# Reading a scatter table back on another queue, and loading the last expert pair one step later

## The chip, the cores and the metric

The kernel runs on one core of a Trainium2 chip. A core has a matrix engine (TensorE, PE in the profile, with its weight loads as PEld), VectorE (DVE), ScalarE (ACT), GpSimd (POOL) and SyncE (SP), which run side by side and wait for each other through semaphores. Transfers between the chip's memory (HBM) and the core's own memory are issued from SP, ACT or POOL and carried by 16 DMA engines. The metric is the device time of one execution in microseconds (us). Lower is better.

## The reference, cut to what matters

One decoder layer over 512 tokens of width 1024: two token-mixing groups, an output projection and a layer norm, and then a mixture of experts with a second layer norm. All that the change touches lies in the experts:

```python
def _hier_moe(h, w_group, b_group, w_expert, b_expert, w1_exp, w3_exp, w2_exp):
    # top-1 of 4 groups, then top-2 of the 8 experts inside that group: `gates`
    ...
    for gi in range(N_GROUPS):
        hid = jax.nn.silu(jnp.einsum('nd,edf->nef', tok, w1_exp[gi])) * jnp.einsum('nd,edf->nef', tok, w3_exp[gi])
        out = out + jnp.einsum('nef,efd->nd', hid * gates[:, gi, :, None], w2_exp[gi])
...
    h = _layer_norm(DEEPNORM_ALPHA * h + ffn, ln2_g, ln2_b)
```

There are 32 experts of width 256, in f32. An expert's w1 and w3 are 2 MB together (its "first weights", tile a), its w2 is 1 MB (its "second weights", tile b). All 96 MB are read from HBM once.

## The kernel before, in words

The 32 experts are worked off as 16 pairs, p = 0 to 15. A pair has 128 slots, 64 for each of its experts, that hold the tokens routed to it. For each pair `gather` fetches the slots' rows by an indirect DMA on GpSimd's queue, `rows` turns them with TensorE and scales them (L1019 on VectorE, L1021 on ScalarE), `ups` multiplies them with the first weights, `hidden` makes silu times product times gate (L1225 on ScalarE, L1226 on VectorE), `turn` turns the result (L1231), and `down` multiplies it with the second weights, in two halves.

What comes out of a pair goes back to its tokens in one of two ways. Pairs 0 to 12 go through `second`: the result is scattered by an indirect DMA on GpSimd's queue (L1316) into a table in HBM, ydram, with two rows for a token. Pairs 13 to 15 (from `LATE_` = 13) go through `combine`: TensorE spreads the result over the tokens, and VectorE adds it to them from the banks (L1214). ydram is read back once, by `back` (L1386), in four DMAs of 1 MB into two tiles a, RT[0] to RT[3], and `gained_rows` (L1394) adds its eight blocks, in 16 additions of 128x512, 12 on VectorE and 4 on GpSimd. RT's tiles are those in which the first weights of pair 13 lay, so they come free with `ups(13)`.

The last pair, `last_pair`, first sums the rows of its second weights (`row_sums`, L1450 on VectorE and L1454 on ScalarE); the sums serve the means of the last layer norm, so that the norm can begin before the last product is out.

The weights come on SP's queue, in the order in which the code issues them. First weights have seven tiles, second weights six. `load_a` and `load_b` load one expert's in one DMA; `load_pair` loads the first weights of two experts in eight DMAs of 512 KB, quarter by quarter. `loads_b(p)` loads the second weights of pair p + 3, at the end of `second(p)`, and for p = 12 those of the last pair, in four halves. Before the change the first weights of the last pair, experts 30 and 31, are issued in step p = 12 (L1333), before `second(11)` issues the second weights of experts 28 and 29.

Two further loads are SP's: the second norm's gain and bias (L1327, at p = 13), of which GpSimd scales the gain (L1328).

The instructions of an engine run in the order of the built program, which a scheduler makes from the code and its dependencies; each waits for the semaphores that stand with it. DMAs of SP's and ACT's queues take turns on eight semaphores, DMAHW0 to DMAHW7, and those of GpSimd's queue on eight others, DMASW0 to DMASW7. A DMA that comes to a semaphore waits, on its issuing engine, until the DMA that held it before has landed.

Of the kernel before, what the change touches and what calls it, by code (L numbers as in the profile page):

```python
# [185 lines left out]
def layer(ctx: ExitStack, tc: tile.TileContext, xT, xt, wb, wad, pc, wla, al, gl, cst, cst2, cst3, abias, wout,  # L186
          lnp, lnt, wr, br, wex, out):
    nc = tc.nc
    PE, V, S, P, SP = nc.tensor, nc.vector, nc.scalar, nc.gpsimd, nc.sync
# [6 lines left out]
    ydram = pdr.tile([1024, 1024], F32, name="ydram")  # L196
# [12 lines left out]
    def T(n, *where):  # L209
        return Buf(n, where or (base,))  # L210
# [20 lines left out]
    def tp(o, i):  # L231
        return inorder(PE.transpose(o, i, late("ident")))  # L232
# [629 lines left out]
    LQ = 15  # L862
# [9 lines left out]
    def load_pair(e, n):  # L872

        for j in (e, e + 1):
            wa_[j] = wa_[j - n] if n else area(f"a{SA[j % len(SA)]}").t
        for q in range(0, 4096, 4096 // HV):
            for j in (e, e + 1):
                SP.dma_start(wa_[j][:, q:q + 4096 // HV], wex[j, :, q:q + 4096 // HV])
# [349 lines left out]
    def turn(pt):  # L1228
        for f in range(2):
            tp(pt[:, 128 * f:128 * f + 128], hd.f[:, 128 * f:128 * f + 128])  # L1230
        S.activation(hdT.f, pt[:, 0:256], AF.Copy)  # L1231
# [61 lines left out]
    def experts_first():  # L1293


        for i in range(4):
            if f"g{i}" not in MODE:
                gains1(i, (P, V))
        after(SP.dma_start(rdram, RR.f), g1, "rows first")
        BB[6] = area("b6")  # L1300
        GA.append(T(1024, BB[6]))
        HTs.append(T(1024, BB[6]))
        P.memset(GA[1].f, 0.0)
        gather(2)
        strict[0], last[1] = True, last[0]

        def second(p):
            Y = YY[p % 2]
            for n in range(2):
                py = B[4 + n]  # L1310
                down(p, n, py)
                if n:
                    V.tensor_copy(Y.g[:, 512:1024], py)
                else:
                    S.activation(Y.g[:, 0:512], py, AF.Copy)
            P.indirect_dma_start(out=ydram, out_offset=bass.IndirectOffsetOnAxis(ap=IDY.i[:, p:p + 1], axis=0),  # L1316
                                 in_=Y.g, in_offset=None, bounds_check=1023, oob_is_err=False)
            loads_b(p)

        for p in range(15):  # L1320
            ph = B[0] if p % 2 or p >= LATE_ else B[6]
            ups(p, HTs[p % 2], ph)
            if p == 13:
                L2.append(area(f"a{SA[4]}"))
                G2 = T(2048, L2[0])
                for j in range(2):
                    SP.dma_start(G2.f[:, 1024 * j:1024 * j + 1024], lnp[2 + j:3 + j, :].to_broadcast([128, 1024]))  # L1327
                P.tensor_scalar(G2.f[:, 0:1024], G2.f[:, 0:1024], -12.0 * K_ ** 5, None, op0=OP.mult)  # L1328
                L2.append(G2)
            late_a = []  # L1330
            if p < HP:
                load_pair(2 * p + 7, 7)
            if LQ <= p + 3 < 16:  # L1333
                load_pair(2 * p + 6, 0)
            for e in range(2 * p + 7, min(2 * p + 9, 2 * LQ) if p >= HP else 0):
                if p < 4 or e == 2 * p + 7:
                    load_a(e, SA)
                else:
                    late_a.append(e)
            hidden(p, ph)  # L1340
            if p < LATE_:
                rows(p + 1, dst=HTs[(p + 1) % 2])
                if p + 3 < 16:
                    gather(p + 3)
                if p > 0:
                    second(p - 1)
                turn(B[3])
            else:
                cbs = lambda k: combine(p - 1, CBS[k]) if p > LATE_ else None
                if p == LATE_:  # L1350
                    second(p - 1)
                    combining()
                if p == 14:
                    back()
                cbs(0)
                turn(B[3])
                cbs(1)
                py = bank((4, 5))
                down(p, 0, py)
                parts(0, py)  # L1360
                cbs(2)
                rows(p + 1, (0,), HTs[(p + 1) % 2])
                cbs(3)
                rows(p + 1, (1,), HTs[(p + 1) % 2])
                if p + 3 < 16:
                    gather(p + 3)
                ot(p)
                py = bank((4, 5))
                down(p, 1, py)
                parts(1, py)  # L1370
                loads_b(p)
            for e in late_a:
                load_a(e, SA)
        gained_rows()
        last_pair(SB, None)

    RT = []

    def back():

        for j in range(2):
            t = T(4096, area(f"a{SA[5 + j]}"))
            for q in range(2):
                RT.append(Part(t, 2048 * q, 2048))
        for i in range(4):
            S.dma_start(RT[i].f, ydram.rearrange("(t r) d -> t (r d)", r=2)[128 * i:128 * i + 128, :])  # L1386

    def gained_rows():
        for i in range(4):
# [239 lines left out]
```

## Time and profile before

| what | us |
|---|---|
| median of 3 runs (772.22 to 775.95) | 775.69 |
| the profiled execution, device time | 777.46 |
| its span from first to last instruction | 775.7 |
| PE busy | 669.7 (86%) |
| PEld busy | 422.9 (55%) |
| DVE busy | 429.2 (55%) |
| ACT busy | 250.2 (32%) |
| POOL busy | 191.3 (25%) |

Of the chain of work that ended last, 53% of the span is PE, 22% DMA and 20% DVE. The first 500 us are token mixing and routing; the experts' steps fill the rest up to some 750 us, and the last norm and the stores the end. From 500 us on the DMA engines are busy nearly throughout, at some 420 GB/s, up to a gap near 690 to 700 us; the weights' last bytes land near 732 us. The steps of the expert pairs can be told in the rows by their waits for DMAs of in_wex, the experts' weights. Busy shares over the whole span say little here: what counts is which wait ends last from 690 us on.

### The profile page before, as it was taken

How to read it: one execution, taken by the hardware profiler on the slowest of the kernel's cores; microseconds unless marked ns; L12 is line 12 of the kernel's file. 1: busy time of each engine (PE TensorE's matmuls, PEld its weight loads, DVE VectorE, ACT ScalarE, POOL GpSimd, SP SyncE). 2: the span in 40 equal slices, each digit the busy share in tenths (PEclk: the TensorE clock that was granted, in tenths of full speed). 3: DMA queues.
4: the chain of work that ended last, by engine and by line, in shares of the span. 5: the costliest groups of instructions: out<-in, count | busy, mean ns of one | idle time of the engine just before them, and what ended most of it. 6: DMA issues, size and time to landing. Idle time of an engine off the chain costs nothing.

```text
span 775.7 us, 9701 instructions
## 1 busy us (share of the span) xinstructions
PE 669.7 (86%) x3420; PEld 422.9 (55%) x3420; DVE 429.2 (55%) x1243; ACT 250.2 (32%) x525; POOL 191.3 (25%) x194
## 2 busy tenths in 40 slices
PE   8988988889889899899999996599998897768780
PEld 2766866777778577667767776233332242223240
DVE  4489579869877985663444498622121121105586
ACT  4333224143333436462453432123131131101230
POOL 3133332262253120310310233511121121100332
PEclk9989999989898999999999996699999899889795
DMA  9611000000000112431538446399999999979602
GB/s 326 246 55 55 28 28 28 27 28 28 28 28 19 50 55 82 125 129 38 207 114 330 185 151 270 118 363 423 422 426 423 423 421 428 423 292 381 270 3 112
DMA packets 28484, 147.18 MB, mean 190 GB/s; under 512 B 5113, under 2 KB 5625, under 8 KB 20492
## 3 DMA queue, kind: packets, MB, share of 16 engines
q1 hardware_dynamic: 23676, 134.61, 44.5%
q0 software_dynamic: 4032, 7.42, 2.6%
q10 hardware_dynamic: 720, 4.46, 1.5%
q8 instruction: 29, 0.48, 0.3%
q14 instruction: 27, 0.22, 0.1%
HBM read 138.38 MB, written 15.36 MB: 198 GB/s over the span
## 4 chain that ended last, share of the span: by engine, by line
PE 53%; DMA 22%; DVE 20%; issue 2%; ACT 1%; POOL 1%; ACTq 0%; SPq 0%; DVEq 0%; POOLq 0%
PE bank L229 49%; DMA a<-in_wex 17%; PE bank L232 4%; DVE base L586 2%; DMA a<-ydram 2%; DVE base L587 2%; DVE a L147 1%; DMA b<-in_wex 1%; DVE base L585 1%; DVE b L603 1%; DMA ydram<-x,base 1%; DVE a L460 1%; DMA a<-in_xT 1%; DVE base L242 1%; DVE base L147 1%
## 5 line engine op out<-in xcount | busy, mean ns | idle before, releaser
L229 PE MATMUL bank<-a,b 128*128 128x512 f32 (+2 forms) x1112 | 286.9, 456 | 12.5 <-DMA a<-in_wex 11.8
L229 PEld LDWEIGHTS bank<-a,b 128*128 128x128 f32 (+1 forms) x1112 | 158.3, 175 | 95.2 <-issue 50.2
L229 PE MATMUL bank<-b,base 128*64 128x512 f32 (+1 forms) x412 | 95.1, 501 | 18.7 <-DMA b<-in_wex 15.1
L337 POOL TENSOR_TENSOR b<-b,b 128x1024 fp32r<-128x1024 f32 x22 | 52.4, 2380 | 131.6 <-ACT b L336 131.2
L229 PE MATMUL bank<-a,base 128*64 128x512 f32 (+3 forms) x308 | 75.6, 570 | 3.8 <-DMA a<-in_wex 3.0
L1226 DVE SCALAR_TENSOR_TENSOR base<-bank,base 128x256 f32<-128x256 f32 x16 | 7.7, 484 | 127.1 <-ACT base L1225 127.0
L229 PEld LDWEIGHTS bank<-b,base 128*64 128x64 f32 (+1 forms) x412 | 41.9, 163 | 58.7 <-issue 42.3
L229 PE MATMUL bank<-a 128*128 128x128 f32 (+4 forms) x248 | 55.6, 333 | 5.4 <-DVE base L243 2.6
L229 PEld LDWEIGHTS bank<-a,base 128*64 128x64 f32 (+2 forms) x308 | 25.9, 143 | 46.0 <-issue 35.3
L1225 ACT ACTIVATE base<-bank 128x256 f32<-128x256 f32 x16 | 6.2, 386 | 135.7 <-PE bank L229 135.7
L229 PEld LDWEIGHTS bank<-a 128*128 128x128 f32 (+1 forms) x248 | 36.0, 190 | 18.2 <-issue 5.3
L229 PE MATMUL bank<-a,a 128*128 128x128 f32 (+2 forms) x200 | 42.6, 346 | 1.4 <-DVE base L243 1.1
L232 PEld LDWEIGHTS bank<-base 128*128 128x128 f32 x156 | 18.3, 145 | 34.3 <-issue 17.8
L229 PEld LDWEIGHTS bank<-a,a 128*128 128x128 f32 x200 | 32.2, 213 | 8.7 <-issue 5.1
L232 PE MATMUL bank<-base 128*128 128x128 f32 x156 | 30.3, 294 | 6.4 <-DVE base L689 5.8
L229 PE MATMUL bank<-base 128*128 128x36 f32 (+4 forms) x136 | 28.3, 344 | 8.0 <-DVE base L1062 2.8
L232 PE MATMUL bank<-base,a 128*128 128x128 f32 x168 | 31.6, 289 | 0.0
L229 PE MATMUL bank<-b,a 128*128 128x128 f32 x192 | 30.1, 299 | 1.7 <-DVE a L645 1.1
L336 ACT ACTIVATE b<-b 128x1024 fp32r<-128x1024 f32 x25 | 26.3, 1055 | 13.7 <-PE bank L229 6.7
L229 PEld LDWEIGHTS bank<-b,a 128*128 128x128 f32 x192 | 27.1, 212 | 4.0 <-DVE a L645 1.9
L1316 POOL DMA_INDIRECT ydram<-x,base x13 | 13.1, 1011 | 64.7 <-ACT base L1231 55.6
L520 DVE CUSTOM_DVE_ANT_0 a<-bank,a 128x512 f32<-128x512 f32 (+3 forms) x32 | 15.6, 489 | 21.0 <-PE bank L232 13.7
(310 smaller groups left out, 1006.1 us busy)
## 6 DMA issues: line engine op xcount, KB each, us to landing
a<-in_wex SPq DMA_DIRECT2D x28, 2048.0 KB, 32.1
b<-in_wex SPq DMA_DIRECT2D x30, 1024.0 KB, 23.6
b<-in_wb SPq DMA_DIRECT2D x25, 512.0 KB, 3.3
a<-in_wex SPq DMA_DIRECT2D x16, 512.0 KB, 9.6
ydram<-base SPq DMA_DIRECT2D x1, 4096.0 KB, 15.1
a<-ydram ACTq DMA_DIRECT2D x4, 1024.0 KB, 12.6
x<-in_wout SPq DMA_DIRECT2D x6, 512.0 KB, 4.7
a<-in_xT SPq DMA_DIRECT2D x8, 256.0 KB, 5.6
```

What stands on the lines that cost most here:

```text
L147: ins = f(*args, **kw)
L229: return inorder(PE.matmul(o, l, r, start=start, stop=stop, skip_group_check=True))
L232: return inorder(PE.transpose(o, i, late("ident")))
L242: V.tensor_tensor(t, y, y, op=OP.mult)
L336: S.activation(hi.f, raw.f, AF.Copy)
L337: (V if 0 < k < 4 else P).tensor_tensor(lo.f, raw.f, hi.g, op=OP.subtract)
L460: V.scalar_tensor_tensor(r.f, r.f, pcol(f"rk{hp}"), k2.f, op0=OP.mult, op1=OP.mult)
L520: V.tensor_tensor_reduce(scs[h].f[:, 0:n], ps[:, 0:n], DT.f[:, 512 - n:512], 1.0, -3e38, op0=OP.add, op1=OP.max, accum_out=mx[:, h:h + 1])
L585: V.stream_shuffle(zt3[:, :, s + 1:], tc3[:, :, s + 1:], [16 * (j // 16) + s for j in range(32)])
L586: V.tensor_tensor(zt3[:, :, s + 1:], zt3[:, :, s + 1:], z3[:, :, s:s + 1].to_broadcast([128, 8, 15 - s]), op=OP.mult)
L587: V.tensor_tensor(z3[:, :, s + 1:], z3[:, :, s + 1:], zt3[:, :, s + 1:], op=OP.add)
L1316: P.indirect_dma_start(out=ydram, out_offset=bass.IndirectOffsetOnAxis(ap=IDY.i[:, p:p + 1], axis=0), in_=Y.g, in_offset=None, bounds_chec ...
```

## The change

Three edits. `load_pair` for the last pair moves from ahead of `hidden(12)` to behind `second(11)`, so that experts 28's and 29's second weights stand ahead of it on SP's queue. `back` moves from step 14 to step 13, right behind `second(12)` and `combining`, and its four DMAs are issued on GpSimd's queue, not ScalarE's. And `loads_b(p)` at the end of steps 13 and 14 goes; for those two p it loads nothing.

```diff
@@ experts_first, loop over p
-            if LQ <= p + 3 < 16:
-                load_pair(2 * p + 6, 0)
...
                 if p > 0:
                     second(p - 1)
+                if p == LQ - 3:
+                    load_pair(2 * LQ, 0)
                 turn(B[3])
...
                 if p == LATE_:
                     second(p - 1)
                     combining()
-                if p == 14:
                     back()
...
                 parts(1, py)
-                loads_b(p)
@@ back
-            S.dma_start(RT[i].f, ydram.rearrange("(t r) d -> t (r d)", r=2)[128 * i:128 * i + 128, :])
+            P.dma_start(RT[i].f, ydram.rearrange("(t r) d -> t (r d)", r=2)[128 * i:128 * i + 128, :])
```

What the built programs make of it is seen at three places. On SP's queue, from the second weights of experts 26 and 27 (tiles b_6) on, this stood before (1024 columns are a quarter of an expert's first weights, 2048 an expert's second weights):

```order
L882 DMA b_6_4147<-in_wex 128x2048 [waits DMAHW0_49,PE_49]
L882 DMA b_6_4149<-in_wex 128x2048 [waits DMAHW2_49,PE_49]
L878 DMA a_3_4170<-in_wex 128x1024 [waits DMAHW4_49]
L878 DMA a_5_4171<-in_wex 128x1024 [waits DMAHW5_49,PE_49]
L878 DMA a_3_4170<-in_wex 128x1024 [waits DMAHW7_49]
L878 DMA a_5_4171<-in_wex 128x1024 [waits DMAHW0_49]
L878 DMA a_3_4170<-in_wex 128x1024 [waits DMAHW1_49]
L878 DMA a_5_4171<-in_wex 128x1024 [waits DMAHW2_49]
L878 DMA a_3_4170<-in_wex 128x1024 [waits DMAHW3_49]
L878 DMA a_5_4171<-in_wex 128x1024 [waits DMAHW4_49]
L882 DMA b_6_4214<-in_wex 128x2048 [waits DMAHW5_49,PE_49]
L882 DMA b_6_4216<-in_wex 128x2048 [waits DMAHW6_49,PE_49]
```

and this stands now:

```order
L882 DMA b_6_4147<-in_wex 128x2048 [waits DMAHW7_49,PE_49]
L882 DMA b_6_4149<-in_wex 128x2048 [waits DMAHW0_49,PE_49]
L882 DMA b_6_4204<-in_wex 128x2048 [waits DMAHW1_49,PE_49]
L882 DMA b_6_4206<-in_wex 128x2048 [waits DMAHW2_49,PE_49]
L878 DMA a_3_4208<-in_wex 128x1024 [waits DMAHW3_49]
L878 DMA a_5_4209<-in_wex 128x1024 [waits DMAHW4_49]
L878 DMA a_3_4208<-in_wex 128x1024 [waits DMAHW5_49]
L878 DMA a_5_4209<-in_wex 128x1024 [waits DMAHW6_49]
L878 DMA a_3_4208<-in_wex 128x1024 [waits DMAHW7_49]
L878 DMA a_5_4209<-in_wex 128x1024 [waits DMAHW0_49]
L878 DMA a_3_4208<-in_wex 128x1024 [waits DMAHW1_49]
L878 DMA a_5_4209<-in_wex 128x1024 [waits DMAHW2_49]
```

Before, SP's DMAs skip the semaphores 1, 3, 6 and 7 once, which the readback on ACT's queue holds in that round, and come to them behind it; now they go round 0 to 7 without a gap, and experts 28's and 29's second weights stand ahead of the last pair's first ones.

On GpSimd the readback stands between the last scatter and the additions now, and the additions wait for semaphores of GpSimd's own queue. L1328, the scaling of the gain, stood between the first and the second addition:

```order
L1316 DMA ydram<-x_3443,base 1024x1024 [waits DMASW2_49,DVE_49,Activation_49]
L1384 DMA a_3_4263<-ydram 128x2048 [waits DMAHW1_49,DMASW3_49,PE_49]
L1384 DMA a_3_4263<-ydram 128x2048
L1384 DMA a_5_4264<-ydram 128x2048 [waits DMAHW2_49,PE_49]
L1384 DMA a_5_4264<-ydram 128x2048 [waits DMASW7_49]
L1392 TENSOR_TENSOR base<-base,a_3_4263 128x512 [waits DMASW4_49,DVE_49]
L1392 TENSOR_TENSOR base<-base,a_3_4263 128x512 [waits DMASW5_49,DVE_49]
L1392 TENSOR_TENSOR base<-base,a_5_4264 128x512 [waits DMASW6_49,DVE_49]
L1392 TENSOR_TENSOR base<-base,a_5_4264 128x512 [waits DMASW7_49,DVE_49]
L1328 TENSOR_SCALAR a_4_4237<-a_4_4237 128x1024 [waits DMAHW6_49,DMAHW3_49]
```

On VectorE eight additions of the readback (L1394, now L1392) stood ahead of the first L1243 of pair 14, with its L1214 ahead of them, and one and three behind. Before, from the last of those L1214 on:

```order
L1214 SCALAR_TENSOR_TENSOR base<-base,bank_71 128x512
L1394 TENSOR_TENSOR base<-base,a_3_4313 128x512 x5
L1394 TENSOR_TENSOR base<-base,a_5_4314 128x512 x3
L1243 TENSOR_TENSOR x_4262<-bank_68,x_4262 128x512
...
L1243 TENSOR_TENSOR x_4262<-bank_69,x_4262 128x512
L1394 TENSOR_TENSOR base<-base,a_5_4314 128x512 x3
L1450 TENSOR_REDUCE a_4_4237<-b_8_4256 128x2
L1450 TENSOR_REDUCE a_4_4237<-b_8_4257 128x2
L1459 TENSOR_TENSOR a_4_4237<-a_4_4237 128x4
L1226 SCALAR_TENSOR_TENSOR base<-bank_64,base 128x256
```

and now:

```order
L1214 SCALAR_TENSOR_TENSOR base<-base,bank_71 128x512
L1392 TENSOR_TENSOR base<-base,a_3_4263 128x512 x2
L1243 TENSOR_TENSOR x_4262<-bank_68,x_4262 128x512
...
L1243 TENSOR_TENSOR x_4262<-bank_69,x_4262 128x512
L1392 TENSOR_TENSOR base<-base,a_3_4263 128x512 x3
L1392 TENSOR_TENSOR base<-base,a_5_4264 128x512 x6
L1448 TENSOR_REDUCE a_4_4237<-b_8_4256 128x2
L1448 TENSOR_REDUCE a_4_4237<-b_8_4257 128x2
L1226 SCALAR_TENSOR_TENSOR base<-bank_64,base 128x256
```

Two additions stand ahead of the first L1243 now, the first of them waiting for RT[0] and the second for RT[1]; one stands between the two L1243 as before (in the rows left out), and nine stand behind the second, ahead of the row sums and of `hidden` of the last pair.

## Rows read from the trace of the kernel before

**Rows 1.** Chain of waits, 560 us on: start us, us, what held it
```profile
690.51 7.64 DMA ydram<-x,base
...
699.54 14.24 DMA a<-ydram
...
713.84 10.52 DMA b<-in_wex
...
724.40 3.68 PE bank L229 x6
```

**Rows 2.** Stages: stretch, its us, engines busy us (instructions), PEclk, DMA share, GB/s
```profile
676.00:681.00 5.00, 4.94 (x12) 1.48 (x14) 0.00 (x0) 0.00 (x0) 0.00 (x0) 0.50 1.01 424
689.00:697.00 8.00, 1.67 (x4) 0.33 (x5) 0.69 (x1) 0.38 (x1) 0.99 (x1) 0.85 0.48 194
697.00:700.60 3.60, 3.60 (x6) 0.75 (x6) 0.49 (x1) 0.00 (x0) 0.00 (x0) 0.50 0.40 116
700.60:712.00 11.40, 11.40 (x55) 4.88 (x55) 3.97 (x9) 3.17 (x7) 0.00 (x0) 0.96 1.00 412
```

**Rows 3.** SP's waits, 680 to 715 us: us in total, times, longest us
```profile
SPq L878 <- DMA a<-ydram: 20.6, 3, 16.0
```

**Rows 4.** Timeline of SP's issues: start us, us from first to last, count
```profile
681.61 29.24 SPq L878 DMA_DIRECT2D a<-in_wex  x8
...
702.95 4.17 SPq L878 DMA_DIRECT2D a<-in_wex  x4
...
715.62 4.10 SPq L1289 DMA_DIRECT2D b<-in_wex  x4
```

**Rows 5.** Timeline of PE: start us, us, form, count [idle before <-releaser]
```profile
676.06 9.07 PE L229 MATMUL bank<-a,b 128*64 128x512 f32 x29 [3.92 <-DMA a<-in_wex]
...
697.00 3.67 PE L229 MATMUL bank<-b,base 128*64 128x512 f32 x6 [1.74 <-DMA b<-in_wex]
...
702.02 1.94 PE L229 MATMUL bank<-b,base 128*64 128x512 f32 x8
...
712.02 1.72 PE L229 MATMUL bank<-x 128*128 128x512 f32 x6
722.01 1.94 PE L229 MATMUL bank<-b,base 128*64 128x512 f32 x2 [8.27 <-DMA b<-in_wex]
...
728.01 1.00 PE L232 MATMUL bank<-base 128*128 128x128 f32 x4
```

**Rows 6.** Timeline of DVE, 711 to 742 us
```profile
714.68 2.96 DVE L1394 TENSOR_TENSOR base<-base,a 128x512 f32<-128x512 f32 x3
...
728.81 0.69 DVE L1243 TENSOR_TENSOR x<-bank,x 128x512 fp32r<-128x512 f32 x1 [8.17 <-ACT x L1242]
...
735.35 0.68 DVE L1243 TENSOR_TENSOR x<-bank,x 128x512 fp32r<-128x512 f32 x1
735.94 1.88 DVE L1394 TENSOR_TENSOR base<-base,a 128x512 f32<-128x512 f32 x3
737.75 2.33 DVE L1450 TENSOR_REDUCE a<-b 128x2 f32<-128x1024 f32 x2
...
740.46 0.48 DVE L1226 SCALAR_TENSOR_TENSOR base<-bank,base 128x256 f32<-128x256 f32 x1
```

**Rows 7.** Timeline of POOL, 701 to 735 us
```profile
714.85 1.64 POOL L1394 TENSOR_TENSOR base<-base,a 128x512 f32<-128x512 f32 x1 [23.34 <-DVE base L1214]
725.79 2.79 POOL L1328 TENSOR_SCALAR a<-a 128x1024 f32<-128x1024 f32 x1 [9.31 <-DMA a<-in_lnp]
```

**Rows 8.** DMA issues, 560 us on: count, KB each, median us to landing
```profile
b<-in_wex SPq DMA_DIRECT2D x4, 512.0 KB, 12.6
...
ydram<-x,base POOLq DMA_INDIRECT x9, 10.8
```

**Rows 9.** DMA queues, 706 to 712 us, then 672 to 674: packets, MB, share
```profile
q10 hardware_dynamic: 218, 1.54, 64.0%
...
q0 software_dynamic: 69, 0.16, 20.0%
```

## The prediction

> **What bounds the kernel now.** I read the chain of waits from its end first. From 740 us back it runs on TensorE and VectorE, and what started that stretch is a transfer: down(14) waited for the second weights of experts 28 and 29 until 724.40, 10.52 us from their issue; that issue, at 713.84, had waited 14.24 us for the readback of ydram, and the readback 7.64 us for the scatter of pair 12 to land, from 690.51 to 698.15 [rows 1]. So a wait for weights that have nothing to do with ydram hangs on the readback.
>
> The stage view shows the price. From 689 to 697 us the DMA engines are busy for 0.48 of the time, from 697 to 700.6 for 0.40, and behind that fully again (1.00) [rows 2]. SP's waits name the cause: L878, the last pair's first weights, waited three times for a landing of the readback, 20.6 us in all and 16.0 in one piece [rows 3]. Its eight issues are spread over 29.24 us from 681.61 on, and the third comes at 702.95 [rows 4], so SP stood from about 687 on at a DMA of the readback that was itself issued only after 698. The reason is the shared round of eight semaphores: the readback on ScalarE's queue holds four of them in the program's order, long before it can start. TensorE then waits 8.27 us and a bit more for experts 28's and 29's second weights, at 722.01 and 724.40 [rows 1, 5].
>
> **What the change does, part by part.** *SP's queue.* With the readback on GpSimd's own semaphores SP's DMAs wait only for earlier DMAs of SP, and these two transfers stand before the last pair's first weights. Experts 26's and 27's second weights are used the moment they land, the latter at 697.00 [rows 5]; two more of 1 MB behind them take 2.5 us each at 0.42 MB/us [rows 2], so 28 and 29 land near 702. TensorE comes to them at 712.02 + 1.72 = 713.7 [rows 5]; 11.7 us of cover. Eight matmuls of down take 1.94 us at the full clock [rows 5], so the turning of pair 15's rows, at 728.01 before [rows 5], starts at 715.7: **12.3 us earlier**. That is the gross gain.
>
> *Where it goes.* The additions of the readback on VectorE were free before: eight of them filled that very stall, from 714.68 on [rows 6]. Now two stand there and nine stand behind the second L1243, ahead of the row sums and of L1226 of the last pair, which TensorE waits for. I follow VectorE. The first two additions start at 714.68 as before. An undisturbed addition takes 0.60 us (1.88 for three, the last one's end included), but the first three took 2.96 [rows 6], 1.08 more, because GpSimd's addition ran from 714.85 to 716.49 beside them [rows 7]. So two are over at 714.68 + 2.96 - 0.60 = 717.0, and L1243, before at 728.81 [rows 6], starts there: 11.8 us earlier. From the first L1243 to the second it was 6.54 us, with one addition within, and the second takes 0.6: 724.1. Nine additions of 0.60 bring 729.5.
>
> *GpSimd's scaling of the gain.* L1328 takes 2.79 us and waits for the gain's landing; before it met an idle VectorE [rows 6, 7]. Now it stands behind all four additions of GpSimd, and falls among the nine. What it costs VectorE no row shows. The nearest is the meeting above: of GpSimd's 1.64 us VectorE lost 1.08, all but 0.56. The same here is 2.79 - 0.56 = 2.2 us; the bounds are 0 (it falls elsewhere) and 2.8. I take 2.2. Two row sums, 2.33 us [rows 6] and 0.1 between, follow: L1226 of the last pair starts at 734.1 instead of 740.46 [rows 6], **6.4 us earlier**.
>
> What a page makes of that term: the Trainium skill, in "SBUF — State Buffer", section "SBUF: two separate sides", says that VectorE and GpSimd share one pair of ports as an exclusive lock, held for a whole instruction, while the other blocks fully. By that rule the term is up to 2.8 us and not 2.2, and the sum below 0.6 us less. The trace agrees so far that VectorE's lengthened addition ended about one addition's length behind GpSimd's.
>
> *The scatter of pair 12* is issued at 690.51 and landed in 7.64 us, with the DMA engines half idle [rows 1, 2]. With that gap filled I take the median of its kind, 10.8 [rows 8]: 701.3. ScalarE's copy of down(13) writes a buffer that the scatter frees; TensorE is done with down(13) at 697.00 + 3.67 = 700.7 [rows 5]. That is **0.6 us lost**, 0 to 1.5.
>
> *The readback.* It starts with the landing of that scatter, at 701.3 instead of 698.15. Before, its first MB had landed by 702.95, 4.8 us later [rows 4], of which 2.5 are the MB at full rate; 2.3 are the start. VectorE needs RT[1] at 715.3. How the DMA engines share between GpSimd's queue and SP's for such a transfer no row shows. From one side: ACT's readback of the same shape, against the same quarters of weights, got 64% and moved 1.54 MB in 6 us [rows 9]; two quarters, 2.1 MB, take 8.2 us, RT[1] lands at 711.8. From the other: GpSimd's indirect transfers got 20%, 0.16 MB in 2 us [rows 9]; then 2.1 MB take 26 us, and RT[1] lands near 730. I take the first: the transfer is the same, only the queue is another. Cover: 3.5 us. GpSimd's queue holds nothing behind the readback but its four additions and L1328, and the additions wait for the same data. The 2 us or so in which ScalarE issued the readback ahead of its copy are off the path, since TensorE was later.
>
> *The rest of the weights.* Their last bytes landed 12.6 us after issues from 715.62 to 719.4, at 732.0 [rows 4, 8]. All bytes are the same, so the end stays at 732.0 at worst; at best it comes (1 - 0.48) x 8.0 + (1 - 0.40) x 3.6 = 6.3 us earlier [rows 2]. The first halves of the last pair's second weights, 2.5 us ahead of the end (723.2 to 729.5), are needed by the row sums at 731.7. The first weights' last quarter lies another 5 us ahead (718.2 to 724.5) and is needed near 726. Both are covered by some 2 us at worst.
>
> *The clock.* TensorE would be ready for L1226 at 740.46 - 11.8 = 728.7 and now waits some 5 us for VectorE. After an idle time of 3.92 us it ran 29 matmuls in 9.07 us [rows 5], with the granted clock at 0.50, the lower level of 1.2 GHz, from 676 to 681 [rows 2]; at 0.24 us each (1.94 for eight) they take 7.0. So 0 to 2.1 us are lost behind such a wait. I take **1.4**, since VectorE carries a part of what follows.
>
> **Sum:** 6.4 - 0.6 - 1.4 = 4.4 us. What follows L1226 is unchanged. The profiled execution took 777.46, 1.77 above the median of 775.69; against its own time 773.1, against the median **771.3 us**, and it is the median that I predict. A difference of 0.5%, 3.9 us, is about what can be told from no change.
>
> **Rivals.** (1) *VectorE is not the bound.* L1328 lands beside work that doesn't touch it, the scatter is no later and the clock holds: 6.4 + 2.2 = 8.6 us, 767.1. For it speaks that the gain's landing may come late; against it, that VectorE has no gap from 711 to 734 in which GpSimd could pass.
>
> (2) *The lock holds back the readback.* VectorE is busy for 3.97 of the 11.4 us from 700.6 to 712 [rows 2]; if each of those holds up GpSimd while it writes the transfer's descriptors, RT[1] comes up to 4 us later, 715.8, and its addition ends 0.5 later; with 2.8 for L1328 that is 4.4 - 0.6 - 0.5 = 3.3, 772.4. The same page and section of the Trainium skill say just this of transfers on GpSimd's queue: while VectorE holds the ports, "GPSIMD is locked out of the shared port pair and **cannot write the descriptors**". No row shows it for a plain transfer.
>
> (3) *Slower: the readback starves on GpSimd's queue.* With the 20% of the indirect transfers RT[1] lands at 730. VectorE then stands in front of the addition, with L1243 and the rows of pair 15 behind it. From RT[1] to L1226 it is two additions' tail of 0.6, then 7.1 + 5.4 + 2.2 + 2.4 = 17.7 us: L1226 at 747.7, 7.2 us later than before, 782.9. Where SP's queue runs dry first, at 726 or so, RT[1] gets the engines sooner, and it is +3 us, 779. It decides from RT[1] at 740.46 - 17.7 = 722.8 on: below that the change still gains. For it: a queue never seen with a plain transfer in this trace. Against: the 64% were had by transfers of the same size, and the 20% by smaller ones against larger.
>
> (4) *The change doesn't do what it says:* SP stands at another semaphore and the second weights come as late as before: 775.7. The order of waits on SP's queue names no readback any more; only a landing that I misread could bring it.
>
> **How the numbers follow.** My forecast, 771.3, own range 769 to 774: 0.50. Rival 1, 767.1: 0.25. Rival 2, 772.4: 0.10. Rival 3: 0.10, most of it slower by over 0.5%, a part (RT[1] between 718 and 724) within it. Rival 4: 0.05. Faster by over 0.5% means below 771.8: 0.30 of the forecast's own, all of rival 1, a little of rival 2: 0.60 with the tails. Slower means above 779.6: 0.07. The rest, 0.33, is within. The range leaves out what rival 1 gains beyond 8.6 us and spread of the runs, and the slower part of rival 3: 766.3 to 776.5.
>
> **What would show it.** SP's L878 with no wait for ydram, and its DMA engines without a gap at 690 to 700. No wait of TensorE for in_wex near 714 to 724. RT[1]'s first addition on VectorE at 715 to 717, and nine additions in a row at 724 to 732 with one or two of them stretched beside L1328. L1226 of the last pair near 734.7, with VectorE, no longer a DMA, in the chain ahead of it; a low granted clock right behind. I am wrong if VectorE waits at its first two additions for a DMA of ydram, if the last pair's `ups` waits for in_wex, or if L1226 comes before 732.

## The result and the profile after

The changed kernel takes 770.49 us (median of 18 runs), the kernel before 775.85 (18 runs): a ratio of **0.9941, 95% interval 0.9922 to 0.9961**, 4.6 us or 0.6% less. The forecast was 771.3 us. The profiled execution takes 770.63 us with a span of 768.9, 6.8 us less than before. One execution each of before, e6, e8 and e10 took 843 to 3455 us; the medians here and below count it, the ratios don't.

The chain of waits from 660 us on (start us, us, what held it):

```profile
664.49 31.22 DMA b<-in_wex
...
695.76 3.68 PE bank L229 x6
...
714.02 2.29 DVE base L1392 x2
...
723.28 5.99 DVE base L1392 x9
729.27 2.25 DVE a L1448 x2
731.53 0.40 DVE base L1226
...
732.63 11.29 PE bank L229 x50
```

Behind the landing of expert 27's second weights, which TensorE uses from 695.76 us on, no transfer is in it any more. The three links of before, scatter, readback and experts 28's and 29's second weights [rows 1], are gone; VectorE's additions and row sums stand in their place.

SP's waits, 670 to 722 us (us in total, times, longest us), and the first weights' issues in the timeline of SP (start us, us from first to last, count):

```profile
SPq L878 <- DMA b<-in_wex: 14.6, 6, 2.9
SPq L878 <- DMA a<-in_wex: 9.1, 2, 4.6
```

```profile
677.99 23.76 SPq L878 DMA_DIRECT2D a<-in_wex  x8
```

No wait for ydram is left: the 20.6 us of [rows 3] have become waits for SP's own earlier loads, 4.6 at the longest where it was 16.0. The eight issues are over at 701.8 us; before they were at 710.9 [rows 4].

Stages (us, then busy us of PE, PEld, DVE, ACT and POOL, granted clock of TensorE, DMA share, GB/s):

```profile
689.00:697.00 8.00, 3.18 (x6) 0.81 (x7) 0.10 (x1) 0.22 (x1) 0.99 (x1) 0.63 0.99 404
697.00:700.60 3.60, 3.60 (x10) 1.47 (x8) 0.94 (x2) 0.68 (x2) 1.97 (x4) 0.50 0.96 383
...
731.00:736.00 5.00, 4.02 (x12) 2.12 (x14) 3.60 (x11) 0.38 (x1) 0.00 (x0) 0.66 0.01 3
```

The gap of the DMA engines is closed: 0.99 and 0.96 busy where [rows 2] has 0.48 and 0.40. The last row is new: TensorE's granted clock is 0.66 behind L1226. In the same stage before, behind its L1226 at 740.46, it was 1.00:

```profile
740.00:745.00 5.00, 5.00 (x22) 2.56 (x22) 3.21 (x12) 1.37 (x3) 0.00 (x0) 1.00 0.01 3
```

TensorE and VectorE (start us, us, form, count, and in brackets the idle time before and what ended it):

```profile
713.00 1.94 PE L229 MATMUL bank<-b,base 128*64 128x512 f32 x8
714.87 0.66 PE L232 MATMUL bank<-base 128*128 128x128 f32 x4
...
731.98 0.65 PE L232 MATMUL bank<-base 128*128 128x128 f32 x2 [3.59 <-DVE base L1226]
```

```profile
713.94 2.37 DVE L1392 TENSOR_TENSOR base<-base,a 128x512 f32<-128x512 f32 x2
716.23 0.68 DVE L1243 TENSOR_TENSOR x<-bank,x 128x512 fp32r<-128x512 f32 x1
...
722.61 0.67 DVE L1243 TENSOR_TENSOR x<-bank,x 128x512 fp32r<-128x512 f32 x1
723.21 6.07 DVE L1392 TENSOR_TENSOR base<-base,a 128x512 f32<-128x512 f32 x9
729.20 2.33 DVE L1448 TENSOR_REDUCE a<-b 128x2 f32<-128x1024 f32 x2
731.45 0.47 DVE L1226 SCALAR_TENSOR_TENSOR base<-bank,base 128x256 f32<-128x256 f32 x1
```

The second product of pair 14, which had waited 8.27 us [rows 5], starts at 713.00 with no wait. L1226 of the last pair comes at 731.45 and not at 740.46 [rows 6]. TensorE waits 3.59 us for it.

### The profile page after: what moved, and what is told of

Its sections match the earlier page's. It is cut to its first block, busy times and chain, and to the rows that moved or that the text cites. A ratio compares the mean times of both kernels' runs of the same rounds, so it can differ in the third digit from the quotient of the medians.

```text
span 768.9 us, 9702 instructions
## 1 busy us (share of the span) xinstructions
PE 668.0 (87%) x3420; PEld 421.4 (55%) x3420; DVE 429.8 (56%) x1243; ACT 250.1 (33%) x525; POOL 193.6 (25%) x198
## 4 chain that ended last, share of the span: by engine, by line
PE 54%; DVE 24%; DMA 17%; issue 2%; ACT 1%; POOL 1%; SPq 0%; DVEq 0%; ACTq 0%; POOLq 0%
PE bank L229 49%; DMA b<-in_wex 13%; PE bank L232 4%; DMA a<-in_wex 4%; DVE base L586 2%; DVE base L587 2%; DVE a L147 1%; DVE base L1392 1%; DVE b L603 1%; DVE base L585 1%; DVE a L460 1%; DMA a<-in_xT 1%; DVE base L1214 1%; DVE base L242 1%; DVE base L688 1%
## 5 line engine op out<-in xcount | busy, mean ns | idle before, releaser
L229 PE MATMUL bank<-b,base 128*64 128x512 f32 (+1 forms) x412 | 92.7, 497 | 8.7 <-DMA b<-in_wex 5.1
L337 POOL TENSOR_TENSOR b<-b,b 128x1024 fp32r<-128x1024 f32 x22 | 52.4, 2382 | 131.5 <-ACT b L336 131.2
L1226 DVE SCALAR_TENSOR_TENSOR base<-bank,base 128x256 f32<-128x256 f32 x16 | 7.7, 483 | 126.2 <-ACT base L1225 126.2
L229 PEld LDWEIGHTS bank<-a,base 128*64 128x64 f32 (+2 forms) x308 | 24.3, 143 | 46.8 <-issue 37.3
L1225 ACT ACTIVATE base<-bank 128x256 f32<-128x256 f32 x16 | 6.1, 384 | 132.3 <-PE bank L229 132.3
L232 PE MATMUL bank<-base 128*128 128x128 f32 x156 | 30.1, 293 | 10.7 <-DVE base L689 5.7
L520 DVE CUSTOM_DVE_ANT_0 a<-bank,a 128x512 f32<-128x512 f32 (+3 forms) x32 | 15.6, 488 | 20.9 <-PE bank L232 13.7
## 6 DMA issues: line engine op xcount, KB each, us to landing
b<-in_wex SPq DMA_DIRECT2D x30, 1024.0 KB, 26.5
```

Of the source, the lines that this page charges most:

```text
L229: return inorder(PE.matmul(o, l, r, start=start, stop=stop, skip_group_check=True))
L337: (V if 0 < k < 4 else P).tensor_tensor(lo.f, raw.f, hi.g, op=OP.subtract)
L520: V.tensor_tensor_reduce(scs[h].f[:, 0:n], ps[:, 0:n], DT.f[:, 512 - n:512], 1.0, -3e38, op0=OP.add, op1=OP.max, accum_out=mx[:, h:h + 1])
L1226: V.scalar_tensor_tensor(hd.f, ph[:, 256:512], GT.f[:, p:p + 1], hd.f, op0=OP.mult, op1=OP.mult)
```

## Experiments

Two theories stood against each other on where the gain comes from. **The order:** experts 28's and 29's second weights must not stand behind the last pair's first weights, whatever queue the readback is on. **The queue:** SP must not stand still for the readback. A third question was what bounds the kernel now.

Executions differ already ahead of the change (expert 27's second weights, used the moment they land, come at 693.7 us in e3 and at 701.2 in e11), so the traces are compared by distances: from L1226 of pair 14 to L1226 of the last pair, from there to the first L147 of the last norm on VectorE, and from L1226 of pair 14 to VectorE's end. Each ratio is against executions of the kernel before beside that run, with medians of 775.77 to 776.71. e4 and e9 are single executions, made for their traces.

| kernel | median us (runs) | ratio to before, 95% | 14 to 15 | 15 to L147 | 14 to end |
|---|---|---|---|---|---|
| before | 775.85 (18) | | 29.2 | 8.4 | 57.4 |
| changed | 770.49 (18) | 0.9941, 0.9922 to 0.9961 | 20.9 | 9.9 | 50.6 |
| e7 changed, again | 772.14 (12) | 0.9948, 0.9921 to 0.9976 | 21.2 | 10.8 | 51.8 |
| e11 changed, again | 771.03 (12) | 0.9933, 0.9914 to 0.9952 | 21.0 | 10.0 | 50.7 |
| e1 order alone | 771.49 (12) | 0.9953, 0.9928 to 0.9978 | 21.2 | 9.8 | 50.8 |
| e2 queue alone | 774.84 (12) | 0.9995, 0.9968 to 1.0021 | 26.5 | 8.4 | 54.7 |
| e9 queue alone, again | 774.06 (1) | | 26.6 | 8.4 | 54.7 |
| e3 nine additions less | 767.15 (8) | 0.9891, 0.9857 to 0.9924 | 17.5 | 8.4 | 45.7 |
| e4 no L1328 | 768.76 (1) | | 20.3 | 10.0 | 50.1 |
| e5 sums behind L1226 | 771.95 (12) | 0.9963, 0.9934 to 0.9992 | 18.9 | 11.6 | 52.4 |
| e6 the same on e1 | 772.07 (12) | 0.9957, 0.9925 to 0.9990 | 18.9 | 10.3 | 50.8 |
| e8 more moved behind | 768.68 (6) | 0.9893, 0.9856 to 0.9931 | 17.2 | 10.7 | 47.7 |
| e10 e8 again | 770.60 (11) | 0.9930, 0.9905 to 0.9954 | 17.2 | 11.1 | 49.9 |
| e12 e8, mended | 767.94 (11) | 0.9896, 0.9866 to 0.9925 | 17.2 | 10.3 | 47.4 |

That `back` stands in step 13 and not 14 needed no run: with the readback on ScalarE's queue and the new order, or on GpSimd's queue and the old order, the built programs of both steps are the same on every engine, up to the names of instructions and buffers.

### e1: the order alone

Upon the kernel before:

```diff
-            if LQ <= p + 3 < 16:
-                load_pair(2 * p + 6, 0)
...
                 if p > 0:
                     second(p - 1)
+                if p == LQ - 3:
+                    load_pair(2 * LQ, 0)
```

> The kernel before with one of the edits: the last pair's first weights are issued behind experts 28's and 29's second weights; the readback stays on ScalarE's queue, so SP and ScalarE still share the eight semaphores, and now the first quarter of the last pair's weights is the one that stands behind the readback. Theory (the false wait costs only because the weights of experts 28 and 29 stand behind it): those weights land near 700 to 703, TensorE does not wait for them at 713, the first quarter is issued near 703 and the eighth lands near 718 to 724, in time for 720 to 726; L1226 of the last pair comes at 731 to 733, the span is 768 to 771, the ratio to before 0.990 to 0.995, as with the whole change. The gap of the DMA engines before 703 stays. Rival (the gain needs the readback off ScalarE's queue, since SP stands still until the readback has landed and the gap in the DMA engines is what costs): the last pair's weights come late, TensorE waits for them at 720 to 726, 772 to 776, ratio 0.996 to 1.000.

SP's waits, 670 to 722 us, and the stages:

```profile
SPq L878 <- DMA a<-ydram: 20.0, 4, 13.2
```

```profile
689.00:697.00 8.00, 1.94 (x2) 0.29 (x2) 0.00 (x0) 0.00 (x0) 0.99 (x1) 0.72 0.82 332
697.00:700.60 3.60, 3.47 (x6) 0.75 (x6) 0.49 (x1) 0.00 (x0) 0.00 (x0) 0.50 0.57 200
```

SP waits for the readback as long as before, 20.0 us, and the DMA engines still have a gap, though a smaller one. TensorE does not wait for the second product of pair 14:

```profile
714.32 1.94 PE L229 MATMUL bank<-b,base 128*64 128x512 f32 x8
```

The time is the changed kernel's, within the intervals, and so nearly are the distances: 21.2 and 50.8 against 20.9 and 50.6. So the false wait itself costs nothing that these runs can tell; what costs is what stands behind it. The first weights of the last pair, issued from 704.66 us on, come in time all the same.

### e2 and e9: the queue alone

Upon the kernel before:

```diff
-            S.dma_start(RT[i].f, ydram.rearrange("(t r) d -> t (r d)", r=2)[128 * i:128 * i + 128, :])
+            P.dma_start(RT[i].f, ydram.rearrange("(t r) d -> t (r d)", r=2)[128 * i:128 * i + 128, :])
```

> The kernel before with the other edit alone: the readback on GpSimd's queue; the last pair's first weights still ahead of experts 28's and 29's second weights. SP has no false wait. Theory (the order on SP's queue matters too, because the readback takes 65% of the DMA engines from 701 to 717 as it did after the whole change): 4 MB are over near 702, the 2 MB of experts 28 and 29 then move at 0.145 MB per us, b28 lands near 712 to 717 and b29 near 718 to 723; TensorE waits for them some 5 to 9 us as before, nine additions fill that wait, L1226 of the last pair is at 734 to 737, the span 770 to 773, ratio 0.994 to 0.998, about half the gain. Rival (the queue alone does it): b29 lands before 713, TensorE doesn't wait, ratio as the whole change's, 0.992 to 0.996, with L1226 near 731.

> The kernel with the readback on GpSimd's queue and the old order of the loads, once more, for a second trace: the first one was of the slowest of its twelve executions, with experts 27's second weights landing at 700.1 us and not near 697. Theory (experts 28's and 29's second weights stand behind 4 MB and share the DMA engines with the readback): they land 23 to 25 us behind expert 27's second weights again, TensorE waits for them 5 to 8 us, L1226 of the last pair comes 26 to 27 us behind L1226 of pair 14 (29.2 before, 20.9 after the whole change); with expert 27's weights at 697 the span is 772 to 774. Rival (the first trace was a disturbed one): they land before TensorE needs them, 21 to 22 us.

TensorE in e9:

```profile
719.12 1.94 PE L229 MATMUL bank<-b,base 128*64 128x512 f32 x2 [6.71 <-DMA b<-in_wex]
```

Without the false wait experts 28's and 29's second weights are issued at 701.38 and 702.64 us in the first trace, and landed only at 722.6 and 725.1; in the second it was 719.0 and 721.5. (Such landings are read from the semaphores' events, sixteen for a transfer; it has landed with the last.) They stand behind the 4 MB, and up to 717 us the readback has 60% and 55% of the engines' time. TensorE waits 6.4 and 6.7 us where it was 8.3. Some 40% of the gain is in the traces (2.7 us less from L1226 of pair 14 to VectorE's end, of 6.8) but it can't be told in the times: 0.9995. Of the 2.7 us 0.65 are lost again behind VectorE's end (last section); the 2 us left would be 0.997, which the interval still holds. In the first trace the landings came 2 to 6 us behind the latest that I expected, though the middle ones of the sixteen parts came at 712.8 and 717.8: I had reckoned with the queue's mean rate and not with its last parts (last section).

### e3 and e4: what bounds the kernel now

e3 leaves nine of VectorE's twelve additions out, e4 GpSimd's scaling of the gain, both upon the changed kernel:

```diff
                     E = P if n and r == 0 else V
                     h = hb[:, i, 512 * n:512 * n + 512]
+                    if E is V and i > 0:
+                        continue
```

```diff
-                P.tensor_scalar(G2.f[:, 0:1024], G2.f[:, 0:1024], -12.0 * K_ ** 5, None, op0=OP.mult)
```

> The changed kernel without the nine additions of the readback's blocks 1 to 3 on VectorE (left out of the computation, as is what they add); all transfers and GpSimd's four additions stay. Theory (VectorE is the bound ahead of the last pair's product since the change, and TensorE's wait of 3.6 us costs a further 1.5 by its lower clock): L1226 moves from 731.45 to 728.5 to 729, where ScalarE's L1225 ends, TensorE waits under 1.5 us there and stays at the full clock; 2.6 + 1.5 = 4 us less, span 764 to 766, ratio to before 0.985 to 0.990. Rival (a transfer of the last pair's weights or the gain's is next and VectorE's additions were nearly free): L1226 stays beyond 730.5, the span 767 to 769.

> The changed kernel without L1328, GpSimd's scaling of the second norm's gain (the gain stays unscaled). What the collision with VectorE's nine additions costs, by itself. The prediction's term, 2.2 us: nine additions in 4.4 us less than... that is L1226 of the last pair at 729.2 instead of 731.45 and 766.7 us of span. By the trace of the changed kernel (one addition of 1.25 instead of 0.68 us beside L1328): 0.57 us, L1226 at 730.9, nine additions in 5.4 to 5.5 us, span 768.3. The rule that GpSimd's whole instruction locks VectorE out, 2.8 us: 728.9 (ScalarE's bound).

The stage behind L1226 in e3, which is at 726.18 there, then the nine additions in e4:

```profile
726.00:731.00 5.00, 4.97 (x21) 2.18 (x20) 3.33 (x11) 2.97 (x9) 0.00 (x0) 1.00 0.01 3
```

```profile
721.91 5.50 DVE L1391 TENSOR_TENSOR base<-base,a 128x512 f32<-128x512 f32 x9
```

e3: L1226 comes 3.4 us sooner, and now it is VectorE that waits, 1.12 us for ScalarE's L1225; TensorE doesn't wait for L1226, the granted clock stays at 1.00, and from L1226 to L147 it is 8.4 us as before the change, not 9.9. VectorE is the bound in the changed kernel, and the wait for it costs TensorE 1.5 us more by its clock. e4: nine additions in 5.50 us where it was 6.07. The collision costs 0.57, a quarter of the 2.2 of the prediction.

### e5 and e6: only the row sums behind L1226

Upon the changed kernel (e6: upon e1). `hidden` hands back its L1226:

```diff
-        for e in range(2):
-            row_sums(e, 0)
         ups(p, HTs[p % len(HTs)], B[0])
-        hidden(p, B[0])
-        row_sums(0, 1)
+        h = hidden(p, B[0])
+        row_sums(0, 1, h)
         cbs(0)
         turn(B[3])
-        row_sums(1, 1)
+        row_sums(0, 0, h)
+        row_sums(1, 1, h)
         cbs(1)
+        row_sums(1, 0, h)
...
-            V.tensor_reduce(rs[:, 2 * e:2 * e + 2], ...)
+            after(V.tensor_reduce(rs[:, 2 * e:2 * e + 2], ...), h, "order")
...
```

> The changed kernel with the row sums of the last pair's second weights ordered behind L1226 of the last pair: the two L1448 on VectorE and the four L1452 on ScalarE, of which one stood ahead of L1225. All work is kept. Theory (VectorE's queue ahead of L1226 is the bound since the change, and TensorE's wait there also costs its clock): L1226 comes where the nine additions end, 2.25 us earlier (20.90 - 2.25 = 18.7 us behind L1226 of pair 14), TensorE waits about 1.3 us instead of 3.6 and keeps the full clock, so from L1226 to the first L147 it is 8.3 to 9.0 us and not 9.9, the reductions fill VectorE's idle time behind it. Together 2.5 to 3.8 us: 767 to 768 by the median, ratio to before 0.987 to 0.991. Rival (VectorE has no room behind L1226, so the 2.3 us come back between L1226 and L147, 10.6 us or more): same as the changed kernel, 770 to 771.

> The row sums behind L1226 as in the run above, but upon the kernel with the order of the loads alone (the readback on ScalarE's queue). Theory (with experts 28's and 29's second weights ahead, it makes no difference on which queue the readback stands): within 0.3% of the run above, 767 to 769, ratio 0.987 to 0.992. Rival (the readback off ScalarE's queue is worth something once VectorE isn't in the way: the last weights land 0.8 us later here and GpSimd's additions meet VectorE's): 1 to 2 us slower than the run above, 768 to 770.

The changed kernel beside them, as it is:

> The changed kernel again, beside these two on the same chip: 770 to 771, ratio 0.992 to 0.996. In its trace L1226 of the last pair again some 21 us behind L1226 of pair 14, and 9.9 us from there to the first L147.

TensorE and the stages in e5, then the control e7:

```profile
736.92 0.40 PE L229 MATMUL bank<-a,base 128*64 128x1 f32 x8 [2.20 <-DVE a L1457]
```

```profile
731.00:736.00 5.00, 3.72 (x16) 1.45 (x14) 5.00 (x10) 2.14 (x6) 0.00 (x0) 1.00 0.01 3
736.00:741.00 5.00, 4.08 (x22) 3.69 (x23) 2.75 (x12) 0.17 (x1) 0.00 (x0) 0.68 0.00 0
```

```profile
731.00:736.00 5.00, 3.54 (x10) 2.01 (x12) 4.08 (x11) 1.10 (x3) 0.00 (x0) 0.50 0.01 3
```

My theory fell here. L1226 is 2.0 to 2.3 us earlier than in the changed kernel's traces, as expected, and the clock holds at first. But the reductions now hold up VectorE behind L1226, TensorE waits 2.2 us for the sums (L1457), and the clock falls there instead (0.68 from 736 to 741 us). The time is the changed kernel's. VectorE is short of time on both sides of L1226. e6 agrees with e5 within the intervals: on which queue the readback stands isn't seen here either, and the gain that was expected of it did not come.

### e8, e10 and e12: VectorE relieved on both sides

All upon the changed kernel. ScalarE makes all row sums and scales the gain, three additions stand behind L1226, and the products of the sums and the means come one step later in TensorE's order (m is L1226, h ScalarE's L1225). No run takes these moves apart.

```diff
-                P.tensor_scalar(G2.f[:, 0:1024], G2.f[:, 0:1024], -12.0 * K_ ** 5, None, op0=OP.mult)
...
+            S.activation(g, g, AF.Copy, scale=-12.0 * K_ ** 5)
...
-        for e in range(2):
-            row_sums(e, 0)
+        row_sums(0, 0, None)
         ups(p, HTs[p % len(HTs)], B[0])
-        hidden(p, B[0])
-        row_sums(0, 1)
+        h, m = hidden(p, B[0])
+        row_sums(1, 0, h)
         cbs(0)
+        if first_down:
+            gained_rows(m)
         turn(B[3])
-        row_sums(1, 1)
+        row_sums(0, 1, h)
+        row_sums(1, 1, h)
         cbs(1)
...
         cbs(2)
-        sums(B[3])
         cbs(3)
-        means(B[3])
+        sums(B[3])
         combine(15, range(PRE))
+        means(B[3])
...
+                    if (m is not None) != bool(i > 0 and r and n):
+                        continue
...
```

> The changed kernel with VectorE's queue ahead and behind L1226 of the last pair made shorter, all work kept: ScalarE makes all eight row sums (two ahead of L1225, six behind) and scales the second norm's gain in place of GpSimd, three of VectorE's nine additions (those of the last halves of the readback's blocks 1 to 3) stand behind L1226, and the sums' and means' products stand one step later on TensorE's queue. Theory (since the change VectorE is the bound on both sides of L1226, and TensorE's clock falls when it waits there): six additions without a collision end 17.3 us behind L1226 of pair 14, near where ScalarE's L1225 ends, L1226 comes at 17.3 to 18 us and not at 20.9 to 21.2, TensorE waits under 1.5 us and keeps its full clock, and from L1226 to the last norm's start it is 8.3 to 9.3 us, not 9.9 to 10.8: 4 to 5.5 us less than the changed kernel, 766 to 768 by the median, ratio to before 0.987 to 0.990. Rival (the sums on ScalarE are late, and TensorE waits for them behind L1226 as it waited 2.2 us when they were put behind L1226 on VectorE; the wait comes back): 769 to 772, no better than the changed kernel.

> The version with a shorter VectorE queue around L1226 once more, since only six of its executions were timed: 766 to 770, ratio to before 0.986 to 0.993, L1226 of the last pair 17 to 18 us behind L1226 of pair 14 and TensorE's granted clock at 1.00 behind it. If the first result was luck, 770 to 772 as the changed kernel.

The changed kernel beside it once more:

> The changed kernel beside it on the same chip: 770 to 772, ratio to before 0.992 to 0.996, L1226 of the last pair 20.9 to 21.3 us behind that of pair 14, and TensorE's granted clock under 0.7 in the 5 us behind it.

TensorE in e10, then the stage in e10 and in e8:

```profile
737.75 0.40 PE L229 MATMUL bank<-a,base 128*64 128x1 f32 x8 [1.17 <-DVE a L1466]
```

```profile
736.00:741.00 5.00, 3.83 (x24) 2.88 (x26) 2.18 (x11) 0.17 (x1) 0.00 (x0) 0.85 0.00 0
```

```profile
736.00:741.00 5.00, 4.73 (x25) 2.63 (x23) 2.66 (x6) 1.29 (x4) 1.37 (x2) 1.00 0.01 2
```

L1226 comes 17.2 us behind that of pair 14 in both traces. But TensorE waited 1.17 us, in both, for the small addition of the sums (L1466), which stood behind four L1214 on VectorE; in e10 the clock fell behind that (0.85 from 736 to 741 us), in e8 it didn't. The 0.9893 of e8, from few runs, was not repeated: 0.9930. e12 takes that addition out of `sums` and writes it behind `cbs(1)`:

```diff
         row_sums(1, 1, h)
         cbs(1)
+        V.tensor_tensor(L34[2][9][:, 0:4], L34[2][9][:, 0:4], L34[2][9][:, 4:8], op=OP.add)
```

> The version with the shorter VectorE queue around L1226, and in it the small addition of the row sums, for which TensorE waited 1.17 us, stands ahead of four L1214 on VectorE and not behind them. Theory (that wait is what took the version's gain back, by 1.2 us of itself and by TensorE's clock behind it, 0.85 from 736 to 741 us in the second trace): from L1226 to the first L147 9.3 to 10.2 us and not 10.7 to 11.1, from the first L147 to VectorE's last 19.9 in place of 21.6, granted clock 1.00 from 731 to 741, together 47 to 48 us from L1226 of pair 14 to VectorE's end (50.6 for the changed kernel, 47.7 and 49.9 for the version); 767 to 769 by the median, ratio to before 0.987 to 0.992. Rival (TensorE then waits as long for the L1214 that free its banks, and the clock falls all the same): 49 to 50 us, 769 to 771, 0.991 to 0.995.

VectorE and the stages behind L1226 in e12:

```profile
723.31 3.69 DVE L1400 TENSOR_TENSOR base<-base,a 128x512 f32<-128x512 f32 x6
727.83 0.49 DVE L1226 SCALAR_TENSOR_TENSOR base<-bank,base 128x256 f32<-128x256 f32 x1 [0.83 <-ACT base L1225]
```

```profile
727.00:731.00 4.00, 4.00 (x18) 1.98 (x18) 3.17 (x8) 3.91 (x13) 0.00 (x0) 1.00 0.07 25
731.00:736.00 5.00, 3.76 (x22) 1.88 (x18) 4.64 (x14) 1.93 (x6) 0.00 (x0) 1.00 0.00 0
```

Six additions run without a collision, VectorE waits 0.83 us for ScalarE's L1225, TensorE doesn't wait for L1226, the clock holds, and it is 47.4 us to VectorE's end. **767.94 us, 0.9896 (0.9866 to 0.9925)**: by its interval faster than the kernel before, and by its median 2.6 to 4.2 us below the changed kernel's three. Its interval overlaps theirs a little, and none of the three ran beside it, so the times alone don't quite show that it is faster than the changed kernel; the distances, 47.4 us against 50.6 to 51.8, say so.

## Why the prediction was right, and where its terms were off

The forecast case came, by its own mechanism: the wait for experts 28's and 29's second weights went, and VectorE and TensorE's clock took a part of the gain back. Of the 6.8 us between the two spans 0.74 lie ahead of the change (L1226 of pair 14 at 710.55 and 711.29); 6.1 are its own, where 4.4 were forecast. By the median it was 5.4, by the ratio 4.6 (3.0 to 6.1). In order, each time of the changed kernel put 0.74 later so that it can be compared:

- **SP's queue, right.** Experts 28's and 29's second weights landed at 698.9 and 701.4, 0.74 later 699.7 and 702.1; forecast was "near 702". Pair 15's rows are turned from 714.87 + 0.74 = 715.6 on; forecast was 715.7.
- **The readback: its share was right, its time by luck.** RT[1] landed at 712.0 + 0.74 = 712.8, forecast 711.8. But two misses cancel in that. The scatter landed 2.5 us ahead of its forecast (698.1 + 0.74 = 698.8 and not 701.3), and from there RT[1] took 14.0 us and not 10.5. The queues, 698 to 704 us and 704 to 716 (packets, MB, share of the engines), and the landings of L1384:

```profile
q1 hardware_dynamic: 482, 1.79, 74.2%
q0 software_dynamic: 71, 0.58, 24.6%
...
q0 software_dynamic: 456, 3.33, 66.8%
q1 hardware_dynamic: 460, 1.67, 34.5%
```

```profile
DMA to landing us min/median/max: 9.6/14.4/19.3
```

  In its first 6 us the readback moved only 0.58 MB. From 704 on GpSimd's queue got 66.8%, ACT's before 64.0% [rows 9]: of the two bounds the transfer of the same shape was the right one. The packets show why: 456 and 460 of them went through, about as many of either queue, and the readback's are of 8 KB, the first weights' of 4 KB. The 20% of [rows 9] were 69 packets of 4 KB and less beside 77 of SP's, most of 8 and 16 KB. So in these stretches the share followed the size of the packets and not the queue.
  Rival 3 was 10 us from its point (722.8). Rival 2, VectorE holding GpSimd up by as much as 4 us (715.8), is not refuted: the slow start would fit it, and it would fit SP's earlier loads too, which had 74.2% of the engines then; no run tells the two apart. It cost nothing here, since VectorE came to RT[1]'s addition only at 714.5.
- **VectorE up to the second L1243, right to 0.1 us:** the first L1243 starts at 716.23 + 0.74 = 717.0 and the nine additions, by the chain, at 723.28 + 0.74 = 724.0; forecast were 717.0 and 724.1.
- **GpSimd's scaling, off by 1.6 us.** This is the term that was mis-sized. I took 2.79 - 0.56 from the meeting of two additions [rows 6, 7]; the nine additions took 5.99 in the chain and not 7.6, and e4 prices the collision at 0.57. The first of the nine took 1.25 us beside L1328, the others ran at their 0.60 while L1328 went on until 725.66. VectorE's first and GpSimd's scaling:

```profile
723.21 1.25 DVE L1392 TENSOR_TENSOR base<-base,a 128x512 f32<-128x512 f32 x1
```

```profile
722.87 2.79 POOL L1328 TENSOR_SCALAR a<-a 128x1024 f32<-128x1024 f32 x1 [1.05 <-DMA b<-in_wex]
```

  The rule that the prediction set beside this term (the Trainium skill, "SBUF — State Buffer", "SBUF: two separate sides": the lock is held for a whole instruction) would have made it 2.8. The runs don't bear that out for this instruction: 0.57 here, and 0.84 in e7.
- **The scatter, off by 0.6.** It landed in 8.2 us (689.9 to 698.1), in a DMA stage that was 0.99 full; I had taken the median of 10.8. ScalarE's copy wasn't held up.
- **The clock, right:** 9.95 us from L1226 to the first L147 and not 8.41, 1.5 lost where 1.4 were forecast; 1.5 (e11) and 2.4 (e7) in the two other traces of the changed kernel. TensorE's wait was 3.59 us where some 5 were forecast. e3 shows that the loss goes when the wait goes.
- **"What follows L1226 is unchanged" was wrong by 0.7 us.** From VectorE's end to the end of the span it is 7.67 us, not 7.00. Half of it (0.33) is in the last step, GpSimd's wait for its queue to drain, which is 2368 ns long before and 2695 after (count, ns min/median/max, first and last start us):

```profile
L1625 POOLq DRAIN  x3: 40/103/2368, 772.5 to 775.4; - x3
```

```profile
L1623 POOLq DRAIN  x3: 40/103/2695, 765.3 to 768.6; - x3
```

Together: 9.01 - 0.74 = 8.27 us earlier at L1226, less 1.54 and 0.67, is 6.1. So rival 1's 8.6 us were nearly there at L1226, for the reason it gave in part (L1328 costs little, the scatter is no later), and the clock and the end took 2.2 back. That the sum came as near as it did owes something to misses on both sides: GpSimd's scaling and the scatter were reckoned 2.2 us too dear, the program's end 0.67 too cheap. I had written that L1226 before 732 would refute me; it came at 731.45, or with the 0.74 at 732.2, just at that line. What was wrong was the size of one term.

What I had not seen is that one of the two edits is enough. The prediction followed them together, and it read the false wait as the cause. e1 shows that with the new order SP may wait as before; e2 and e9 show that without it the wait's removal brings 2.7 us in the traces and nothing that the times can tell.

## What to carry to other kernels

Here the queue that stood still cost only what was queued behind the waiting transfer and was needed first: before a wait is removed, look whether an order in which nothing urgent stands behind it does the same. When a stall goes, the work that filled it for nothing can land on the path, here six of VectorE's additions, and the engine that now waits for it may lose a second time by its clock. Moving the row sums only to the far side of the waited-for instruction (e5) gave nothing; giving them and the scaling to ScalarE and moving three additions besides (e12) brought 47.4 us in place of some 51.

## What the runs showed that I had not expected

- **The last parts of a transfer lag, and a gap lets them catch up.** In the changed kernel thirteen of the sixteen parts of the last pair's eighth quarter had landed by 712.8 us, the last two at 720.4 and 721.5. From the middle part to the last it was 6 us for expert 29's second weights, and up to 15 while the readback shared the engines. Before, it was 7.5 us for the second of the eight quarters (692.5 and 700.0), ahead of the DMA engines' gap, and 0.2 for the readback's first MB behind it (702.7 and 702.9); in e1 the eighth quarter had 2.5 (719.8 and 722.3). So the gap that the change closes was partly time in which the last parts caught up. Whether they are always the same engines' parts these events don't tell.
- **The readback on GpSimd's queue costs 0.7 us at the end of the program.** The last drain is 2.37 us in before, e1 and e6, with the readback on ScalarE's queue, and 2.70 in the eleven traces with it on GpSimd's; from VectorE's end to the span's it is 6.97 to 7.00 us against 7.63 to 7.84. Where the other half of the difference comes from is open. e12 upon the order of e1 might save that; it wasn't tried.
- **The same wait doesn't always cost the same.** TensorE waited 3.83 us for L1226 both in e1 and in e7; from L1226 to L147 that cost 1.4 us in e1 (granted clock 0.66 in the 5 us from 732.6) and 2.4 in e7 (0.50 in the 5 us from 731.5). The same two waits of 0.47 and 1.17 us further on went with a lower clock in e10 (0.85 from 736 to 741 us) and not in e8 (1.00).
